# Making the low part of 109 weight tiles with an adding transfer instead of on VectorE

## The chip, the cores and the metric

One core of one Trainium2 chip runs the whole program. The metric is the device time of one execution in microseconds; lower is better.

## The reference

Two layers of a diffusion backbone over 256 latent tokens and 256 context tokens, width 1024, batch 1, all in float32. A layer normalises and modulates its tokens, then runs three branches on the result and merges them:

```python
q, k, v = h @ w_q, h @ w_k, h @ w_v          # 8 heads, each with two 64-wide halves
a = softmax(q1 k1) - lam * softmax(q2 k2)    # differential attention, axial rotary on latents
y_b = rms_norm(a @ v) @ w_attn_out
y_a = silu(layer_norm(conv31(glu(h)))) @ w_conv_out
y_c = (window_mean(h @ w_p) - h @ w_p) @ w_group @ w_pool_out
m = sum(sigmoid(h @ w_g + b_gate) * (y_a, y_b, y_c))
x = x + gate1 * rms_norm(m @ w_out)
x = x + gate2 * rms_norm((silu(h2 @ w1) * (h2 @ w2)) @ w_ffn_out)
```

The first layer does this for latent and context tokens (512 columns). The second needs the context tokens only for its keys and values, so most of its products have 256 columns.

## The kernel before

The weights lie in HBM as 302 units of 128 x 1024 float32 (512 KB), in the order of their use: the first layer's values, queries and keys (units 0 to 23), the gated convolution input "glu" (24 to 31), pooling, the three merges (to unit 76), output projection "wo" and feed-forward "fi", "fo" (77 to 150), and then the second layer, which begins with glu (151 to 158), values, queries and keys (159 to 182).

TensorE multiplies float32r operands here, so each float32 operand is kept as a pair: hi, its rounding to float32r, and lo, the rest. A product is three matmuls, hi x hi, hi x lo and lo x hi (`mm3`, L331 to L333). `prep` makes the pair of one unit: SyncE's queue loads the unit into `raw` (L295), ScalarE writes `hi = Copy(raw)` (L347) and VectorE writes `lo = raw - hi` (L348). `split` is also the helper that splits activations, so L347 and L348 stand for those too; the weight units are the rows with the names hi, lo and raw.

There are four buffers each of raw, hi and lo. `unit` calls `prep` for up to five units ahead of the one that it hands out, so a pair is made as soon as one of the four buffers of each kind is free: hi and lo come free with the last matmul of an earlier unit, raw with the last reader of the raw tile.

Nearly every changed unit is 24 matmuls (8 blocks of the contraction, three matmuls each). Where the tokens are stationary (`v_proj`, and the output projections), the weights are the moving operand, 512 columns wide. The first layer's second `v_proj` and both of the second layer take all four units at once and walk over the token tiles, so all four must be there early.

VectorE also has the softmax maxima (L704), the rotary products, the lo of every activation, and the 31 taps of the depthwise convolution (L832). In the second layer the taps are handed out in portions (`step`) between the query and key products of the attention. ScalarE has the exponentials, the copies out of PSUM and the hi of everything. GpSimd has small parts: one rotary product (L611), the lo of the keys in the second layer (L622), one channel group's taps (L829), the pooling windows and the merges' additions (L1015); it issues no transfer. `mod_close` (L400 on) turns rows of the modulation product into a gate by way of VectorE's L348 and TensorE.

The program is written in Tile: a planner walks through the instructions with its own estimate of their times and fixes each engine's order at build time, so a change of one instruction can move others. Each engine then runs its list in order and waits on semaphores.

Of the kernel before, what the change touches and what calls it, by code (L numbers as in the profile page):

```python
# [21 lines left out]
AF = mybir.ActivationFunctionType  # L22
ALU = mybir.AluOpType
# [24 lines left out]
COL_P = 4096  # L48
# [154 lines left out]
class Net:  # L203
# [85 lines left out]
    def prep(self):  # L289
        nc = self.nc  # L290
        key = self.order[self.pi]
        n = 512 if key[0] == "grp" else UW
        x = "x" if key[1] == DEPTH - 1 and key[0] in self.XK and self.pi % self.XN == 0 else ""
        raw = self.t("raw" + x, [P, UW])
        dma = nc.sync.dma_start(out=raw[:, :n], in_=self.io["w"][self.pi, :, :n])  # L295
        if x:
            self.after(self.last_dma, dma)
        self.last_dma = dma
        hi = self.t("hi" + x, [P, UW], F32R)
        lo = self.t("lo" + x, [P, UW], F32R)  # L300
        a, _ = self.split(hi[:, :n], lo[:, :n], raw[:, :n])
        if self.gate is not None and self.pi >= self.limit:
            self.after(self.gate[0], a)
            if self.pi >= self.limit + 3:
                self.gate, self.limit = None, len(self.order)
        self.prepped.append((key, hi, lo))
        self.pi += 1
# [988 lines left out]
```

## Time and profile before

| | |
|---|---|
| three runs | 1557.73 us median, 1556.97 to 1563.15 |
| profiled execution | 1556.86 us, of which the span is 1555.1 |
| TensorE busy | 1518.8 us, 98% of the span |
| VectorE, ScalarE, GpSimd busy | 974.6, 752.0 and 192.4 us |
| transfers | 236.70 MB, 152 GB/s mean |
| granted TensorE clock, mean | 0.996 of full speed |

Busy time is measured per engine inside the span, which runs from the first to the last instruction; the 1.76 us between span and execution lie around it. Matmuls overlap in the array, so a stretch in which TensorE is all busy may still hold fewer matmuls than it could.

### The profile page before, as it was taken

To read this page: it belongs to the slowest core of one execution; us is meant where nothing else is said; L and a number is where in the kernel's file an instruction comes from. 1 tells how busy PE (TensorE), PEld (TensorE's weight loads), DVE (VectorE), ACT (ScalarE), POOL (GpSimd) and SP (SyncE) were. 2 spreads that over 40 slices of the span, in tenths; PEclk is the share of its full clock that TensorE was granted. 3 is DMA by queue.
4 is the path that set the end of the run, shared out by engine and by line. 5 is a ranking of instruction groups with operands and counts; after the bars stand their busy time and mean duration, and the time that the engine had idled before them with its cause. 6 is when DMAs were issued, how large, how long until landed. Compare 5 with 4: busy or idle time off the path is not lost.

```text
span 1555.1 us, 22537 instructions
## 1 busy us (share of the span) xinstructions
PE 1518.8 (98%) x8616; PEld 1253.0 (81%) x8616; DVE 974.6 (63%) x1580; ACT 752.0 (48%) x1284; POOL 192.4 (12%) x216
## 2 busy tenths in 40 slices
PE   6999999999999999999999999998999999999998
PEld 3788878878777688877888888887789799799986
DVE  4588787999964347334333222899998656665554
ACT  5467768532353236322222221865677665554443
POOL 0000100630131100000000000054134212000000
PEclk9999999999999999999999999999999999999999
DMA  9643342232335644446322235534244675556553
GB/s 344 207 121 99 105 133 95 71 123 91 132 116 186 205 141 149 148 169 203 100 95 95 95 118 167 198 106 144 93 137 158 240 254 192 188 177 210 182 189 110
DMA packets 81693, 236.70 MB, mean 152 GB/s; under 512 B 9648, under 2 KB 18480, under 8 KB 81584
## 3 DMA queue, kind: packets, MB, share of 16 engines
q1 hardware_dynamic: 81584, 235.26, 45.7%
q8 instruction: 67, 1.10, 0.3%
q14 instruction: 42, 0.34, 0.1%
HBM read 223.69 MB, written 5.24 MB: 147 GB/s over the span
## 4 chain that ended last, share of the span: by engine, by line
PE 71%; DVE 9%; issue 1%; ACT 1%; DVEq 0%; ACTq 0%
PE psg L332 11%; PE psg L331 11%; PE psg L333 11%; PE pss L331 10%; PE pss L333 10%; PE pss L332 10%; DVE O L832 2%; PE pso L332 2%; PE pso L333 2%; PE pso L331 2%; DVE lo L348 1%; DVE Q L832 1%; PE pss L380 1%; PE pst L380 1%; PE pss L701 1%
## 5 line engine op out<-in xcount | busy, mean ns | idle before, releaser
L347 ACT ACTIVATE hi<-raw 128x1024 fp32r<-128x1024 f32 x299 | 315.2, 1056 | 528.7 <-PE psg L332 162.3
L348 DVE TENSOR_TENSOR lo<-raw,hi 128x1024 fp32r<-128x1024 f32 x299 | 375.5, 1256 | 294.0 <-ACT hi L347 290.0
L331 PE MATMUL psg<-H,hi 128*128 128x512 f32 (+1 forms) x864 | 300.0, 349 | 1.3 <-ACT H L347 0.9
L332 PE MATMUL psg<-H,hi 128*128 128x512 f32 (+1 forms) x864 | 299.4, 347 | 0.7 <-DVE H L348 0.7
L333 PE MATMUL psg<-H,lo 128*128 128x512 f32 (+1 forms) x864 | 299.5, 347 | 0.0
L331 PE MATMUL pss<-H,hi 128*128 128x256 f32 (+1 forms) x704 | 236.7, 337 | 0.1
L332 PE MATMUL pss<-H,hi 128*128 128x256 f32 (+1 forms) x704 | 235.3, 334 | 0.0
L333 PE MATMUL pss<-H,lo 128*128 128x256 f32 (+1 forms) x704 | 234.6, 333 | 0.0
L331 PEld LDWEIGHTS psg<-H,hi 128*128 128x128 f32 x864 | 162.1, 188 | 28.9 <-issue 3.2
L332 PEld LDWEIGHTS psg<-H,hi 128*128 128x128 f32 x864 | 162.4, 188 | 25.1 <-issue 3.8
L333 PEld LDWEIGHTS psg<-H,lo 128*128 128x128 f32 x864 | 162.4, 188 | 22.1 <-issue 1.8
L331 PEld LDWEIGHTS pss<-H,hi 128*128 128x128 f32 x704 | 132.2, 188 | 17.1 <-issue 2.5
L333 PEld LDWEIGHTS pss<-H,lo 128*128 128x128 f32 x704 | 133.8, 190 | 14.9
L332 PEld LDWEIGHTS pss<-H,hi 128*128 128x128 f32 x704 | 133.0, 189 | 14.0
L832 DVE SCALAR_TENSOR_TENSOR Q<-Q,perm,Q 128x482 f32<-128x482 f32 (+14 forms) x120 | 99.4, 828 | 2.5
L829 POOL TENSOR_TENSOR O<-O,tp 128x241 f32<-128x241 f32 (+14 forms) x30 | 24.6, 820 | 473.6 <-ACT tp L827 471.5
L707 ACT ACTIVATE E<-pss,st 128x512 f32<-128x512 f32 (+1 forms) x96 | 58.7, 613 | 38.1 <-DVE st L704 33.0
L1087 DVE TENSOR_TENSOR S<-pss,S 128x256 f32<-128x256 f32 (+1 forms) x43 | 23.8, 554 | 80.8 <-PE pss L333 80.8
L331 PE MATMUL psg<-V,hi 128*128 128x512 f32 (+1 forms) x192 | 64.5, 341 | 3.3 <-ACT S L1003 3.1
L1015 POOL TENSOR_TENSOR O<-O,S 128x512 f32<-128x512 f32 (+1 forms) x32 | 43.9, 1373 | 188.2 <-DVE S L1013 169.4
L332 PE MATMUL psg<-V,hi 128*128 128x512 f32 (+1 forms) x192 | 65.0, 339 | 0.8 <-DVE V L348 0.8
L333 PE MATMUL psg<-V,lo 128*128 128x512 f32 (+1 forms) x192 | 64.5, 337 | 0.0
(373 smaller groups left out, 2638.5 us busy)
## 6 DMA issues: line engine op xcount, KB each, us to landing
raw<-w SPq DMA_DIRECT2D x297, 512.0 KB, 3.4
mod<-wmod SPq DMA_DIRECT2D x66, 512.0 KB, 4.6
A<-wmod SPq DMA_DIRECT2D x18, 256.0 KB, 5.4
O<-wmod SPq DMA_DIRECT2D x16, 256.0 KB, 4.9
QD<-T SPq DMA_DIRECT2D x32, 128.0 KB, 2.4
E<-wmod SPq DMA_DIRECT2D x14, 256.0 KB, 5.3
row<-b_mod SPq DMA_DIRECT2D x24, 128.0 KB, 4.0
xs<-Q SPq DMA_DIRECT2D x12, 256.0 KB, 2.1
```

The costliest lines, as they stand in the source:

```text
L331: mm(out, sh, mh, start=start, stop=False)
L332: mm(out, sh, ml, start=False, stop=False)
L333: return mm(out, sl, mh, start=False, stop=stop)
L347: return (self.nc.scalar.activation(hi, src, AF.Copy), (lo_eng or self.nc.vector).tensor_tensor(out=lo, in0=src, in1=hi.bitcast(F32), op=A ...
L348: (lo_eng or self.nc.vector).tensor_tensor(out=lo, in0=src, in1=hi.bitcast(F32), op=ALU.subtract))
L380: ins = nc.tensor.matmul(ps[32 * kk:32 * kk + 32, 0:256], self.cc[:, k, :], raws[k], start=(k < 4), stop=(k >= 4), tile_position=(0, 32 * ...
L701: nc.tensor.matmul(pss[j][:, :n], q[a][:, j, qt * P:(qt + 1) * P], k[:, j, k0:NT], start=(a == 0), stop=(a == 1))
L707: nc.scalar.activation(e[:, :n], pss[j][:, :n], AF.Exp, bias=mx[:, j:j + 1], accum_out=ss[:, j:j + 1])
L829: nc.gpsimd.tensor_tensor(out=accs[i][:, a:b], in0=accs[i][:, a:b], in1=t, op=ALU.add)
L832: last[0] = nc.vector.scalar_tensor_tensor(out=av, in0=uv, scalar=prm[:, w:w + 1], in1=av, op0=ALU.mult, op1=ALU.add)
L1015: nc.gpsimd.tensor_tensor(out=m[:, :n], in0=m[:, :n], in1=gs[:, :n], op=ALU.add)
L1087: nc.vector.tensor_tensor(out=s[:, :n], in0=pg[:, :n], in1=s[:, :n], op=ALU.mult)
```

## The change

For 109 units, all of the first layer up to the end of its merges (0 to 76) and the second layer's glu, values, queries and keys (151 to 182), the pair is made in another way. ScalarE writes hi as before, and then also writes -raw, rounded in the same way, into lo, which so holds -hi. GpSimd then issues a transfer that reads the same unit from HBM a second time and adds it to what lies in lo, so that lo ends as raw - hi. VectorE has no part in it. The other 193 units stay as they were.

```diff
         hi = self.t("hi" + x, [P, UW], F32R)
         lo = self.t("lo" + x, [P, UW], F32R)
-        a, _ = self.split(hi[:, :n], lo[:, :n], raw[:, :n])
+        if key[0] in ("wo", "fi", "fo") or key[1] > 0 and not (
+                key[0] == "v" or key[0] == "in" and key[2] < COL_P):
+            a, _ = self.split(hi[:, :n], lo[:, :n], raw[:, :n])
+        else:
+
+            a = nc.scalar.activation(hi[:, :n], raw[:, :n], AF.Copy)
+            nc.scalar.activation(lo[:, :n], raw[:, :n], AF.Copy, scale=-1.0)
+            nc.gpsimd.dma_start(out=lo[:, :n], in_=self.io["w"][self.pi, :, :n],
+                                accum_op=ALU.add)
```

## Rows read from the trace of the kernel before

**Rows 1.** The page, part 1: the span, and busy time, share, instructions of TensorE.
```profile
span 1555.1 us, 22537 instructions
PE 1518.8 (98%) x8616; PEld 1253.0 (81%) x8616; DVE 974.6 (63%) x1580; ACT 752.0 (48%) x1284; POOL 192.4 (12%) x216
```

**Rows 2.** Windows by stage: length, busy time (instructions) by engine, clock, DMA share, GB/s.
```profile
55.00:280.00 225.00, 224.43 (x1140) 179.95 (x1139) 172.46 (x345) 152.28 (x295) 13.12 (x20) 1.00 0.38 115
...
280.00:440.00 160.00, 158.91 (x707) 125.32 (x706) 153.84 (x185) 54.08 (x74) 54.47 (x63) 1.00 0.32 107
...
1015.00:1040.00 25.00, 25.00 (x119) 20.60 (x118) 24.00 (x34) 16.51 (x33) 17.32 (x22) 1.00 0.20 66
1040.00:1120.00 80.00, 72.71 (x383) 58.28 (x382) 79.68 (x155) 45.56 (x91) 26.08 (x25) 0.98 0.35 113
```

**Rows 3.** TensorE's waits from 55 to 545 us: total, times, longest (the longest row of four).
```profile
PE psg L332 <- DVE V L348: 0.8, 1, 0.8
```

**Rows 4.** TensorE's waits in the second layer's attention, 1015 to 1215 us.
```profile
PE pst L400 <- DVE rows L348: 4.2, 2, 2.3
PE psg L331 <- ACT S L1003: 3.1, 1, 3.1
PE pss L701 <- POOL K L622: 1.7, 2, 1.5
PE pss L701 <- DVE QL L348: 0.9, 1, 0.9
```

**Rows 5.** Groups by form, whole span: count, busy us, mean ns, idle before.
```profile
L348 DVE TENSOR_TENSOR lo<-raw,hi 128x1024 fp32r<-128x1024 f32 x297 | 374.1, 1260 | 294.0 <-ACT hi L347 290.0 <-DMA raw<-w 0.2 <-PE pso L332 0.2
L347 ACT ACTIVATE hi<-raw 128x1024 fp32r<-128x1024 f32 x297 | 314.0, 1059 | 524.2 <-PE psg L332 157.7 <-issue 148.9 <-PE pss L332 95.2
```

**Rows 6.** VectorE's weight splits from 1040 to 1120 us.
```profile
L348 DVE TENSOR_TENSOR lo<-raw,hi 128x1024 fp32r<-128x1024 f32 x12 | 15.1, 1256 | 0.0
```

**Rows 7.** VectorE's and ScalarE's weight splits from 55 to 280 us.
```profile
L348 DVE TENSOR_TENSOR lo<-raw,hi 128x1024 fp32r<-128x1024 f32 x30 | 36.6, 1221 | 6.2 <-ACT hi L347 5.7 <-PE pso L332 0.2
...
L347 ACT ACTIVATE hi<-raw 128x1024 fp32r<-128x1024 f32 x29 | 30.7, 1057 | 10.7 <-PE psg L332 8.1 <-PE pso L333 2.1
```

**Rows 8.** A GpSimd addition by form; the page's weight loads with us to landing.
```profile
L1015 POOL TENSOR_TENSOR O<-O,S 128x512 f32<-128x512 f32 x16 | 25.1, 1569 | 112.5 <-DVE S L1013 96.8 <-DMA E<-wmod 9.5 <-DVE perm L426 6.2
...
raw<-w SPq DMA_DIRECT2D x297, 512.0 KB, 3.4
```

**Rows 9.** Weight loads (L295) issued in the first 60 us: us to landing.
```profile
DMA to landing us min/median/max: 3.4/6.5/8.4
```

**Rows 10.** Windows of the start and just behind it, columns as in Rows 2.
```profile
15.00:50.00 35.00, 33.05 (x211) 18.37 (x212) 15.81 (x41) 16.26 (x27) 0.00 (x0) 1.00 1.02 369
50.00:55.00 5.00, 5.00 (x24) 4.04 (x23) 3.09 (x6) 2.62 (x5) 0.00 (x0) 1.00 0.17 58
```

**Rows 11.** Timeline of unit 0: start, length; its lo, a load's issue, its first matmul with lo.
```profile
18.39 1.22 DVE L348 TENSOR_TENSOR lo<-raw,hi 128x1024 fp32r<-128x1024 f32 x1
...
21.56 0.33 SPq L295 DMA_DIRECT2D raw<-w  x1
...
23.75 0.39 PE L332 MATMUL psg<-lo,H 128*128 128x512 f32 x1
```

**Rows 12.** Timeline of unit 15, last of the first layer's second values: its lo, first matmuls with lo.
```profile
117.78 1.21 DVE L348 TENSOR_TENSOR lo<-raw,hi 128x1024 fp32r<-128x1024 f32 x1
...
120.10 0.63 PE L332 MATMUL psg<-lo,H 128*128 128x512 f32 x2
```

**Rows 13.** Timeline of units 155 (glu) and 162 (values) of the second layer: lo, first matmul.
```profile
998.65 1.23 DVE L348 TENSOR_TENSOR lo<-raw,hi 128x1024 fp32r<-128x1024 f32 x1 [1.26 <-ACT hi L347]
...
1003.60 0.28 PE L333 MATMUL psg<-H,lo 128*128 128x256 f32 x1
...
1016.93 1.22 DVE L348 TENSOR_TENSOR lo<-raw,hi 128x1024 fp32r<-128x1024 f32 x1 [0.40 <-ACT hi L347]
...
1019.73 0.39 PE L332 MATMUL psg<-lo,H 128*128 128x512 f32 x1
```

## The prediction

> **What bounds the kernel now.** I began with the page's busy times. TensorE is busy 1518.8 of 1555.1 us; VectorE, which the change relieves, 974.6 [rows 1]. So 36 us of the span are open to any gain at all, and work taken off VectorE is worth only what it takes out of TensorE's waits. I looked for those by stage. From 55 to 440 us, the first layer's attention and half of its merges, TensorE is busy 224.43 of 225 and 158.91 of 160 us, although VectorE is busy 77% of the one stretch and 96% of the other [rows 2]. The longest total among its waits there is 0.8 us [rows 3]. A saturated VectorE costs nothing in that layer. The second layer's attention is different: from 1040 to 1120 us VectorE is busy 79.68 of 80 us and TensorE 72.71, and the granted clock has fallen to a mean of 0.98 of full speed [rows 2]. TensorE waits there for VectorE's rows of a gate (4.2 us), for ScalarE's sigmoid (3.1), for GpSimd's lo of the keys (1.7) and for VectorE's lo of the queries (0.9) [rows 4]. That is where VectorE is worth something.
>
> **What the change removes.** 109 of VectorE's splits at 1260 ns are 137 us [rows 5]. In the first layer I give them nothing, because TensorE hardly waits (above). In the stretch from 1040 to 1120 us, 12 of them take 15.1 of VectorE's 79.68 us [rows 6, 2], so its backlog shrinks by a fifth. Of the waits in rows 4, those for VectorE and GpSimd come to 4.2 + 1.7 + 0.9 = 6.8 us. They are waits for a result behind other work in an engine's list, so a shorter list should cut them and not end them: I take half, 3.4 us. The bounds are nothing, and all of rows 4 with the clock, 9.9 + 0.02 x 80 = 11.5 us.
>
> **What it adds on ScalarE.** A second pass per unit at 1059 ns [rows 5], 115 us in all. From 55 to 280 us some 30 units bring 32 us [rows 7] to the 152.28 that ScalarE has [rows 2]: 184 of 225 us, 82%. VectorE stands at 77% in that stretch today and TensorE does not wait for it, so I take nothing; what covers it is the work of another head that TensorE has beside each softmax. Without that cover, 82% could cost some 5 us. The raw buffer now comes free after two ScalarE passes (2.12 us) where it took a ScalarE and a VectorE pass (2.32 and VectorE's queue), so SyncE's loads start no later.
>
> **What it adds in the chain of one unit.** Before, lo is there 1.22 us after VectorE starts on it [rows 11]. Now come ScalarE's pass (1.06), GpSimd's issue, and a transfer of 512 KB that reads HBM, reads lo and writes lo. The kernel before issues no transfer from GpSimd, so both parts are bounded. The issue: no less than SyncE's 0.33 [rows 11], no more than GpSimd's addition of 512 columns, 1.57 [rows 8]; I take 1.0, about midway. The landing: a weight load's median of 3.4 us [rows 8] below, the slowest load of the crowded start, 8.4 [rows 9], above; I take 1.5 x 3.4 = 5.1, for three streams where a load has two. So lo is later by 1.06 + 1.0 + 5.1 - 1.22 = 5.9 us, with bounds of 3.6 (0.33 and 3.4) and 9.8 (1.57 and 8.4).
>
> The Trainium skill, "DMA: Bandwidth & Descriptors", section "Anatomy of one DMA", puts a transfer from GpSimd at 2.0 us plus its bytes at 436 GB/s; no run here shows one. An estimate by that page is 3.2 us for issue and landing together, 3.0 us of delay in place of 5.9, and a sum near no change.
>
> **Where the delay reaches TensorE.** With four buffers a unit has up to three units of TensorE's time between its buffer and its use, and mostly that covers it. I laid each unit's lo beside its first matmul and looked for less than 5.9 us:
> - Unit 155, in the second layer's glu, where a unit has 256 columns and so takes half the time: lo ends at 999.88, its first use is at 1003.60 [rows 13]. 3.7 us of cover, 5.9 - 3.7 = 2.2 us lost.
> - Unit 162, the last of the four that the value product takes together right behind: lo ends at 1018.15, used at 1019.73 [rows 13]. 1.6 us of cover, 4.3 us lost.
> - Unit 15, the same place in the first layer: lo ends at 118.99, used at 120.10 [rows 12]. 1.1 us of cover, 4.8 us short. Here attention's matmuls are interleaved and the planner can move some ahead: I take half, 2.4.
> - The start. From 15 to 50 us the transfer engines are full (share 1.02, 369 GB/s), then nearly idle (0.17) [rows 10]. Four units' second reads, 4 x 524,288 bytes at 369 GB/s, are 5.7 us in front of the modulation weights that TensorE needs next. Unit 0 has 4.1 us of cover (19.61 to 23.75) [rows 11] and loses 1.8 more. Between nothing, if the four fit in gaps of the queue, and 7.5 I take 4.
>
> That the start pays for second reads on another queue at all is read from its full share [rows 10]. The Trainium skill, "DMA: Bandwidth & Descriptors", section "Issuing engines are not separate DMA queues", says the same of all transfers: whichever engine issues them, they run on the same 16 engines. By that rule the start would pay the whole 5.7, and the sum be 1.7 higher.
>
> Elsewhere the second reads have room: 30 units at 1.42 us are 43 us of the 225 from 55 to 280, a share of 0.38 that becomes 0.57 [rows 2, 10].
>
> GpSimd's list gets an instruction that waits for ScalarE's second pass. Behind it stand the rotary products, the keys' lo and the merges' additions, and for these wait VectorE and then TensorE's scores. I price that at nothing beyond the issue, since TensorE is a head ahead; the rest of it is in the upper bound.
>
> **The sum.** Lost: 2.2 + 4.3 + 2.4 + 4 = 12.9 us. Gained: 3.4. Net 9.5 on the profiled execution's 1556.86 (span 1555.1): 1566 us. The median of the runs, 1557.73, lies 0.9 above that execution, well inside what I can resolve. I take 0.5%, 7.8 us, as about what a measurement of this kernel can tell from no change.
>
> **The rivals.**
> - *VectorE's relief decides* (the other side). Place: 1040 to 1120 us. If the taps no longer crowd out the rows and the splits, all of rows 4 and the lost clock come back, 11.5 us. With a delay of 3.6 the losses are unit 162's 2.0 and half of unit 15's 2.5, 3.2 together: 8.3 us faster, 1548.6. At a delay of 5.9 this gain is eaten (12.9 lost), so it decides below about 5. For it: VectorE's 79.68 of 80. Against: 3.1 of rows 4 hang on ScalarE, which gets more work.
> - *A slow transfer.* At 9.8 us of delay, by crowding or by GpSimd's list, unit 155 loses 6.1, unit 162 8.2, unit 15 8.7 and the start 5.7 + 5.7: 34.4 us, 1591. For it: loads of the same size do take 8.4 when the engines are full. Against: they are not full at units 155 and 162.
> - *The transfer is hidden anyway.* At 3.6 us the same 3.2 us are lost and half of the waits, 3.4, come back: 1556.7. The Trainium skill's figure in "DMA: Bandwidth & Descriptors" (above) would lead here.
>
> **How the numbers follow.** I give the forecast case 0.40, with a range of its own from 1560 to 1573; about two thirds of that is slower by over 0.5%, the rest within. The slow transfer gets 0.15, all slower. The hidden transfer gets 0.19, all within. VectorE's relief gets 0.26, all faster. So faster 0.26, within 0.5% 0.13 + 0.19 = 0.32, slower 0.27 + 0.15 = 0.42. The range reaches from a little beyond the relief, 1546, to the slow transfer, 1591; what lies outside is the stronger half of the one and the worse part of the other, under 2 in 10.
>
> **What would show it.** VectorE's weight splits fall from 302 to 193, ScalarE's passes over raw rise by 109, and GpSimd has 109 issues whose row gives the landing: near 5.1 us if I am right, near 3.4 or over 8 for the rivals. TensorE should show new waits, for ScalarE or a transfer of lo, at 23 us, near 1003 and 1019, and at the first layer's second values. From 1040 to 1120 us VectorE should drop from 79.68 of 80 to some 65, and the wait for rows should shrink. I am wrong if TensorE's idle time at those four places does not grow, if its waits in the second attention go altogether, or if a stage that I priced at nothing (ScalarE in the first attention, GpSimd's list) holds the difference.

## The result and the profile after

The changed kernel takes 1612.4 us (median of four runs, 1610.28 to 1612.57) where the kernel before takes 1558.05: a ratio of 1.034, interval 1.032 to 1.036. It is 54 us slower, outside my range and beyond the worst of my rivals (1591). The profiled execution is 1610.28 us with a span of 1608.5.

The page of the changed kernel, parts 1, 3 (queue: packets, MB, share of 16 engines), 5 and 6 (last column: us from issue to landing):

```profile
span 1608.5 us, 22739 instructions
PE 1536.8 (96%) x8616; PEld 1260.1 (78%) x8616; DVE 856.3 (53%) x1471; ACT 851.4 (53%) x1394; POOL 276.8 (17%) x325
...
q1 hardware_dynamic: 81584, 235.26, 43.5%
q0 software_dynamic: 15696, 56.89, 19.1%
...
L308 POOL DMA_DIRECT2D lo<-w x109 | 95.4, 875 | 899.5 <-ACT lo L307 437.4
...
raw<-w SPq DMA_DIRECT2D x297, 512.0 KB, 4.0
lo<-w POOLq DMA_DIRECT2D x108, 512.0 KB, 8.3
...
QD<-T SPq DMA_DIRECT2D x32, 128.0 KB, 6.4
```

VectorE did lose its work: 974.6 us [rows 1] became 856.3. The span grew by 53 us. Of these, 35 are idle time of TensorE (72 us outside its busy time, where 36 were), and 18 are the same 8616 matmuls taking longer. The mean granted clock fell from 0.996 to 0.989 of full speed; by an estimate from these means and the two spans that is worth about 11 us, part of it in idle time. Two lines name suspects. Queue q0 carries the adding transfers: 56.89 MB for 19.1% of the 16 engines' span, while q1 moves 235.26 MB for 43.5%. Per MB that is 0.336% against 0.185%. And lo lands 8.3 us after its issue, not the 5.1 that I took.

Windows of the changed kernel, in the columns of [rows 2] (busy time by engine, granted clock, DMA share, GB/s):

```profile
15.00:50.00 35.00, 30.42 (x189) 14.51 (x185) 10.35 (x34) 20.18 (x32) 4.45 (x5) 0.95 1.05 350
55.00:280.00 225.00, 210.48 (x1024) 166.64 (x1023) 125.39 (x281) 160.68 (x290) 38.14 (x48) 0.98 0.73 181
280.00:440.00 160.00, 154.74 (x718) 121.19 (x718) 135.65 (x187) 87.22 (x127) 60.48 (x83) 0.98 0.74 170
1085.00:1165.00 80.00, 70.72 (x367) 57.10 (x366) 71.29 (x141) 52.18 (x97) 33.61 (x36) 0.94 0.69 172
```

From 55 to 280 us TensorE is busy for 210.48 of 225 us, where it had 224.43 [rows 2]: this stage, which I had called safe, loses most. Its DMA share went from 0.38 to 0.73; I had written 0.57. The last line is the stretch of [rows 2] at 1040 to 1120, moved by the 45 us that TensorE is late there: VectorE is relieved (71.29 of 80, before 79.68), yet TensorE does less than before. Its longest waits there are 6.6 us for a gate that VectorE makes (G, L418, next table) and 2.2 us for an exponential.

TensorE's longest waits in the changed kernel, whole span:

```profile
PE pss L709 <- ACT E L715: 11.2, 3, 6.0
...
PE psg L341 <- DMA lo<-w: 7.9, 6, 2.5
PE pss L709 <- DVE G L418: 6.6, 1, 6.6
PE pst L777 <- ACT row L355: 3.7, 2, 2.6
PE pst L778 <- DVE row L356: 2.9, 2, 2.7
```

The largest is no wait for a weight: the scores (L709) wait for an exponential on ScalarE (L715), 6.0 us at once. The timeline of the changed kernel around it (start, length, engine, line; in brackets the idle time ahead and its releaser) shows why:

```profile
95.70 3.05 SPq L640 DMA_DIRECT2D QD<-T  x4
95.82 0.88 POOL L308 DMA_DIRECT2D lo<-w  x1 [0.65 <-ACT lo L307]
...
106.94 1.06 ACT L355 ACTIVATE QH<-QD 128x1024 fp32r<-128x1024 f32 x1 [9.23 <-DMA QD<-T]
107.91 0.67 ACT L715 ACTIVATE E<-pss,st 128x512 f32<-128x512 f32 x1
108.03 1.22 DVE L356 TENSOR_TENSOR QL<-QD,QH 128x1024 fp32r<-128x1024 f32 x1 [9.13 <-ACT QH L355]
108.72 0.58 PE L709 MATMUL pss<-K,QH 128*128 128x256 f32 x1 [5.97 <-ACT E L715]
```

At 95.70 SyncE issues the four small transfers that stack a head's rotated queries on chip (QD, L640; in the kernel before L632). At 95.82 GpSimd issues an adding transfer. ScalarE's next instruction in its list splits the queries and waits 9.23 us for them. Behind it in the list stands the exponential, ready but not reachable, and for that TensorE's next scores wait 5.97 us. Three engines stand still behind 512 KB of queries that are already on the chip. The rest of the 11.2 us are two such waits, of 3.0 and 2.2 us, each behind a query split that waited for its transfer (4.85 and 3.91 us). While the four transfers were under way the transfer engines were full (next to last number of a row):

```profile
98.00:100.00 2.00, 2.00 (x10) 1.61 (x9) 0.90 (x3) 0.00 (x0) 0.25 (x1) 1.00 0.99 202
100.00:102.00 2.00, 2.00 (x11) 1.66 (x10) 0.00 (x0) 0.00 (x0) 0.00 (x0) 1.00 1.03 221
102.00:104.00 2.00, 0.75 (x4) 0.27 (x2) 0.00 (x0) 0.00 (x0) 0.00 (x0) 1.00 1.09 247
```

That this is crowding shows in the transfers of one stretch, 50 to 150 us, in both kernels. Before:

```profile
q1 hardware_dynamic: 4467, 11.47, 38.1%
...
raw<-w SPq DMA_DIRECT2D x13, 512.0 KB, 3.7
mod<-wmod SPq DMA_DIRECT2D x4, 512.0 KB, 4.2
QD<-T SPq DMA_DIRECT2D x16, 128.0 KB, 2.4
```

After:

```profile
q1 hardware_dynamic: 5062, 12.29, 40.6%
q0 software_dynamic: 1811, 6.57, 34.5%
...
raw<-w SPq DMA_DIRECT2D x12, 512.0 KB, 9.7
lo<-w POOLq DMA_DIRECT2D x11, 512.0 KB, 8.7
QD<-T SPq DMA_DIRECT2D x16, 128.0 KB, 8.0
mod<-wmod SPq DMA_DIRECT2D x2, 512.0 KB, 15.1
```

q1 costs the same per MB as before (3.3% each), the adding queue 5.25%. Every other transfer of the stretch lands later: queries 8.0 us instead of 2.4, weights 9.7 instead of 3.7. Over the whole stretch the engines have idle time (mean share 0.75), but a small transfer meets the load of its own few microseconds, and that was full.

To see where the time goes I laid the first matmul of each unit beside that of the kernel before, both measured from the start of the span. TensorE is late by these us (columns: the changed kernel and experiments told below):

```
unit                     before at  after  e1    e2    e4    e5    e6    e16
1   values                  37.8    +8.1  -2.2  +5.3  +1.2  +1.0  +7.7  -0.3
8   keys, first head        84.6    +9.6  -3.9  +3.0  +1.2  +2.3  +5.7  +1.0
12  second values          114.0   +21.1  -6.1  +4.3  +2.4 +15.3  +5.8  +1.2
15                         119.6   +21.9  -6.9  +4.5  +2.4 +15.5  +5.8  +1.1
38  first merge            314.4   +26.1  +3.4  +7.2  +2.4 +21.4  +9.7  +5.2
39                         321.4   +33.5  +3.2 +11.1  +2.7 +29.0 +18.2 +14.3
78  output projection      553.5   +37.1  +1.0 +10.8  +2.7 +35.2 +21.0 +20.0
151 second layer, glu      990.3   +37.9  +1.8 +11.6  +3.5 +35.9 +21.8 +20.8
158                       1012.9   +43.8  +9.2 +18.3 +20.0 +49.5 +28.0 +34.6
162 last of four values   1019.5   +45.0  +9.2 +18.6 +19.9 +49.0 +27.9 +34.1
301 last unit             1546.0   +53.3  +9.5 +17.6 +25.3 +61.9 +31.9 +40.2
```

In the changed kernel: 8.1 us at the start, 11.5 between units 8 and 12, where the first heads' queries are stacked, 7.4 at one place, unit 39, 5.9 in the second glu, 8.3 after unit 162, and some 12 in small pieces between. Not every step of the table is a loss: work that the planner put elsewhere shows too, as in e1, where the -6.9 at unit 15 is +0.1 at unit 16.

### The profile page after: what moved, and what is told of

Its sections match the earlier page's. It is cut to its first block, busy times and chain, and to the rows that moved or that the text cites. A ratio compares the mean times of both kernels' runs of the same rounds, so it can differ in the third digit from the quotient of the medians.

```text
span 1608.5 us, 22739 instructions
## 1 busy us (share of the span) xinstructions
PE 1536.8 (96%) x8616; PEld 1260.1 (78%) x8616; DVE 856.3 (53%) x1471; ACT 851.4 (53%) x1394; POOL 276.8 (17%) x325
## 3 DMA queue, kind: packets, MB, share of 16 engines
q1 hardware_dynamic: 81584, 235.26, 43.5%
q0 software_dynamic: 15696, 56.89, 19.1%
## 4 chain that ended last, share of the span: by engine, by line
PE 71%; DMA 8%; DVE 8%; issue 6%; ACT 5%; SPq 1%; POOL 0%; DVEq 0%; ACTq 0%; POOLq 0%
PE psg L339 11%; PE psg L341 11%; PE psg L340 11%; PE pss L339 9%; PE pss L341 9%; PE pss L340 9%; DVE O L840 2%; PE pso L340 2%; DMA QD<-T 2%; DMA lo<-w 2%; PE pso L339 2%; PE pso L341 2%; DVE Q L840 2%; DMA mod<-wmod 1%; PE pst L388 1%
## 5 line engine op out<-in xcount | busy, mean ns | idle before, releaser
L355 ACT ACTIVATE hi<-raw 128x1024 fp32r<-128x1024 f32 x190 | 200.2, 1056 | 372.3 <-issue 153.7
L356 DVE TENSOR_TENSOR lo<-raw,hi 128x1024 fp32r<-128x1024 f32 x190 | 235.5, 1242 | 240.1 <-ACT hi L355 235.5
L308 POOL DMA_DIRECT2D lo<-w x109 | 95.4, 875 | 899.5 <-ACT lo L307 437.4
L339 PEld LDWEIGHTS psg<-H,hi 128*128 128x128 f32 x864 | 164.1, 190 | 35.4 <-issue 5.8
L340 PEld LDWEIGHTS psg<-H,hi 128*128 128x128 f32 x864 | 164.1, 190 | 24.6 <-issue 2.5
L306 ACT ACTIVATE hi<-raw 128x1024 fp32r<-128x1024 f32 (+1 forms) x109 | 114.4, 1050 | 114.7 <-PE psg L340 65.9
L307 ACT ACTIVATE lo<-raw 128x1024 fp32r<-128x1024 f32 (+1 forms) x109 | 113.7, 1043 | 9.6 <-PE pso L340 5.7
L715 ACT ACTIVATE E<-pss,st 128x512 f32<-128x512 f32 (+1 forms) x96 | 58.7, 613 | 18.5 <-DVE st L712 14.1
```

What stands on the lines that cost most here:

```text
L306: a = nc.scalar.activation(hi[:, :n], raw[:, :n], AF.Copy)
L307: nc.scalar.activation(lo[:, :n], raw[:, :n], AF.Copy, scale=-1.0)
L308: nc.gpsimd.dma_start(out=lo[:, :n], in_=self.io["w"][self.pi, :, :n], accum_op=ALU.add)
L339: mm(out, sh, mh, start=start, stop=False)
L340: mm(out, sh, ml, start=False, stop=False)
L355: return (self.nc.scalar.activation(hi, src, AF.Copy), (lo_eng or self.nc.vector).tensor_tensor(out=lo, in0=src, in1=hi.bitcast(F32), op=A ...
```

## The experiments

Each ratio is to the kernel before, with its 95% interval; the kernel before lies between 1556.9 and 1558.4 us in all of them. Edits are to the changed kernel unless said otherwise.

**The transfer taken away, and made plain.** e1 and e2 part ScalarE's second pass, the plain second read and the adding.

```diff
 e1
-            nc.gpsimd.dma_start(out=lo[:, :n], in_=self.io["w"][self.pi, :, :n],
-                                accum_op=ALU.add)
 e2
-            nc.gpsimd.dma_start(out=lo[:, :n], in_=self.io["w"][self.pi, :, :n],
-                                accum_op=ALU.add)
+            nc.gpsimd.dma_start(out=lo[:, :n], in_=self.io["w"][self.pi, :, :n])
```

> Leaves out the adding transfer alone: lo stays at -hi, so its time counts and its numbers do not. If the transfers cost the 54 us, by their own lateness or by what they hold up, this runs at 1548 to 1560 us. If ScalarE's second pass or the new order of the lists costs it, this stays above 1590.

> The same transfer as a plain copy: it writes the unit over lo and adds nothing. The bytes from HBM, the queue and GpSimd's list are those of the change. If the adding makes a packet take twice as long on the transfer engines (0.19 of the engines' span for 56.89 MB, against 0.435 for 235.26 MB), about half of the loss goes: 1575 to 1590 us. If the number of bytes or GpSimd's list is what costs, it stays at 1605 to 1612.

e1: 1565.94 us, 1.0049 [1.0033, 1.0064], between its two expectations. e2: 1576.6 us, 1.0120 [1.0104, 1.0136]. The page of e2, the plain transfer's queue and landings over the whole span:

```profile
q0 software_dynamic: 15696, 56.89, 10.6%
...
lo<-w POOLq DMA_DIRECT2D x108, 512.0 KB, 5.1
...
QD<-T SPq DMA_DIRECT2D x32, 128.0 KB, 3.4
```

The same packets and bytes from the same queue take 10.6% of a span of 1572.8 us when copied, 167 us, and 19.1% of 1608.5 when added, 307 us: 1.84 times. Adding instead of copying costs 35.8 of the 54 us. The plain landing, 5.1 us, is by chance the one I had estimated for the adding transfer.

Without any transfer the changed kernel is still 8 us slower than before, and the table puts 7 of them between units 151 and 158. There TensorE waits once for the glu's sigmoid on ScalarE, 4.7 us. TensorE's waits in e1:

```profile
PE psg L337 <- ACT S L793: 6.0, 2, 4.7
PE pss L707 <- POOL K L628: 3.8, 2, 2.5
```

**No lo at all.** e9 leaves out ScalarE's second pass too and reads hi in lo's place (the line that takes lo's tile moves into the other branch, not shown).

```diff
-            nc.scalar.activation(lo[:, :n], raw[:, :n], AF.Copy, scale=-1.0)
-            nc.gpsimd.dma_start(out=lo[:, :n], in_=self.io["w"][self.pi, :, :n],
-                                accum_op=ALU.add)
+            lo = hi
```

> Leaves out the making of lo for the 109 units altogether: no VectorE split, no second ScalarE pass, no transfer, and the matmuls read hi in its place, so its time counts and its numbers do not. It is what VectorE's relief would be worth for nothing. If the second attention waits for VectorE: 1545 to 1553. If nothing does: 1556 to 1560, and the 8 us by which the kernel without the adding transfer (1566) stood above before are ScalarE's second pass.

1550.59 us, 0.9943 [0.9922, 0.9963]. VectorE's relief, had for nothing, is worth 7.8 us against the kernel before of the same runs (6 to 12 by the interval), and the waits for lo, which e9 has none of, are in that. From e9 to e1, ScalarE's second pass costs 15.4.

**ScalarE's pass given to VectorE.** -raw is written by VectorE, the rest as changed.

```diff
-            nc.scalar.activation(lo[:, :n], raw[:, :n], AF.Copy, scale=-1.0)
+            nc.vector.tensor_scalar(lo[:, :n], raw[:, :n], -1.0, None, op0=ALU.mult)
```

> The changed kernel with -raw written into lo by VectorE (one input) instead of a second ScalarE pass. Against the run without any lo (1551), ScalarE's pass alone stood at 1566, 15 us. If that pass is dear because of its place in ScalarE's list, about 10 us come back here: 1600 us. If its cost only looked so because nothing else was late in those runs, no change: 1608 to 1614.

1612.22 us, 1.0352 [1.0336, 1.0367]: the total does not change. With the adding transfer there, the place of the pass does not matter to it; TensorE's longest waits of e13 are now for lo and for the keys that GpSimd makes:

```profile
PE psg L341 <- DMA lo<-w: 11.6, 8, 2.9
PE pss L709 <- POOL K L630: 10.1, 2, 6.5
```

So the 15.4 of e1 and the transfer's cost are not two terms that can be moved one by one: with ScalarE freed of the pass, other waits took its place.

**Queries without transfers.** e6 stacks them by four copies on VectorE; e7 does that in the kernel before, as a control.

```diff
-                nc.sync.dma_start(out=d[64 * r:64 * r + 64, j, :n],
-                                  in_=q[64 * j:64 * j + 64, :n])
+                nc.vector.tensor_copy(d[64 * r:64 * r + 64, j, :n],
+                                      q[64 * j:64 * j + 64, :n])
```

> The changed kernel with the queries stacked by four VectorE copies of 64 partitions instead of four transfers (QD). Those small transfers took 6.4 us to land where they took 2.4 before. If the adding transfers cost by holding them up, 14 to 20 us come back: 1592 to 1598. If the lateness of lo itself or ScalarE's list is what costs, 1608 to 1614.

> The control for the run with copied queries: the same four copies in the kernel before. Their transfers were not late there, so no theory gives them more than a few us: 1553 to 1562.

e6: 1590.13 us, 1.0199 [1.0172, 1.0226], 22 us less than the changed kernel. e7: 1556.62 us, 0.9993 [0.9982, 1.0003]. The copies are worth nothing before and 22 us after, so the queries' late transfers hold that much. The table shows where: between units 8 and 12 e6 loses 0.1 us where the changed kernel lost 11.5. TensorE's waits of e6 from 55 to 320 us hold no scores:

```profile
PE psg L339 <- ACT S L795: 1.2, 1, 1.2
PE psg L341 <- DMA lo<-w: 0.8, 1, 0.8
```

e6 also takes the queries' own 6 MB off the engines, so its 22 us hold a little relief of the other transfers too.

**The same copies with the plain transfer.** e15 joins the edits of e6 and e2.

> Copied queries (1590 with adding transfers) and the transfer as a plain copy that adds nothing. If what is left of the loss is again the longer packets, through lo itself and the modulation loads, it goes to 1566 to 1576, near the 1566 of the kernel without the transfer. If the query transfers were all that the longer packets hurt, it stays at 1584 to 1592.

1573.0 us, 1.0107 [1.0092, 1.0122]. With a plain transfer the copies give 3.6 us (from e2), with the adding one 22. And adding costs 17.1 us with copied queries (1573.0 to 1590.13), 35.8 without: half of what adding costs reaches TensorE through the queries.

**Another queue for the queries.** Is it SyncE's list that holds them up? e14 issues them from ScalarE's queue.

```diff
-                nc.sync.dma_start(out=d[64 * r:64 * r + 64, j, :n],
+                nc.scalar.dma_start(out=d[64 * r:64 * r + 64, j, :n],
```

> The changed kernel with the query-stacking transfers (QD) issued from ScalarE's queue instead of SyncE's, everything else the same. If they are late because they stand behind weight loads in SyncE's queue, they land in 2.5 to 4 us again and 10 to 20 us come back: 1592 to 1602. If they are late because the 16 engines are shared with the adding packets, they stay at 5 us or more and the time at 1605 to 1616.

1621.96 us, 1.0420 [1.0396, 1.0444], slower than either theory expected. The page's landing row for them:

```profile
QD<-T ACTq DMA_DIRECT2D x32, 128.0 KB, 6.1
```

6.1 us against 6.4: from issue to landing, the queue makes no difference. The Trainium skill, "DMA: Bandwidth & Descriptors", section "Issuing engines are not separate DMA queues", says that all of them end on the same 16 engines and interleave there, and this row agrees. Why it is 10 us slower was not followed up; the issues now stand in ScalarE's list.

**One stage alone.** e3 changes units 0 to 76, e4 151 to 182, e8 36 to 76, each by its own bounds in `prep`, as in e4:

```diff
-        if key[0] in ("wo", "fi", "fo") or key[1] > 0 and not (
-                key[0] == "v" or key[0] == "in" and key[2] < COL_P):
+        if not 151 <= self.pi <= 182:
```

> Only units 0 to 76 by transfer, the second layer as before. In the changed kernel TensorE was 37 us late when the first layer's merges were done, so if the stages add up: 1595 us.

> Only units 151 to 182 by transfer, the first layer as before. The rest of the lateness, 16 us, if the stages add up: 1574 us. If VectorE's relief in the second attention were worth something by itself, under 1570.

> Only units 36 to 76, the first layer's merges, by transfer. No query transfers run there, units have 8 to 18 us of cover, and VectorE is at 95%. By the lateness of lo alone nothing is lost: 1556 to 1560. In the changed kernel TensorE fell 11 us further behind over this stretch (7.4 of it where the second half of the heads is normalised), so if the transfers do that by themselves: 1565 to 1570.

e3: 1594.11 us, 1.0236 [1.0218, 1.0254], 36.0 more than before, as expected. e4: 1582.32 us, 1.0165 [1.0143, 1.0187], 24.2 more, where the table's 16 (53.3 less 37.1) had been expected. e8: 1569.13 us, 1.0080 [1.0063, 1.0097], 11.7 more. Alone the second layer loses 16.5 us in its glu, against 5.9 in the changed kernel. The timeline of e4 has the reason, two long waits of TensorE, and its windows the granted clock (the next to last three numbers of a row are clock, DMA share, GB/s):

```profile
1013.25 0.58 PE L340 MATMUL psg<-H,lo 128*128 128x256 f32 x1 [4.10 <-DMA lo<-w]
1023.30 0.58 PE L338 MATMUL psg<-H,hi 128*128 128x256 f32 x1 [3.67 <-ACT S L794]
```

```profile
1000.00:1010.00 10.00, 9.15 (x77) 8.94 (x76) 3.11 (x11) 8.98 (x15) 1.72 (x2) 1.00 0.75 207
1010.00:1020.00 10.00, 6.38 (x30) 6.18 (x30) 2.34 (x5) 4.33 (x7) 1.73 (x2) 0.66 1.05 269
1020.00:1030.00 10.00, 6.70 (x36) 6.02 (x36) 2.57 (x5) 7.07 (x12) 0.86 (x1) 0.66 0.75 179
```

The waits come to 7.8 us. Behind each of them the granted clock stood at 1.2 GHz while TensorE was busy for 11.6 us in all, which by an estimate is 5.8 us more. Some 3 of the 16.5 us stay unexplained. e8's extra includes 6.1 us at unit 39.

**The start undone.** e5 gives units 0 to 3 back to VectorE; e16 does so with copied queries.

```diff
+        if not (4 <= self.pi <= 76 or 151 <= self.pi <= 182):
```

> The changed kernel with units 0 to 3 back on VectorE, so that no adding transfer runs while the start fills the transfer engines. TensorE was 8 us late at unit 1 in the changed kernel: if the start's share is paid in full, 1604 us. If later waits swallow it, 1609 to 1612.

> Copied queries and units 0 to 3 back on VectorE. Undoing the start alone changed nothing (1615 against 1612). If a later wait for queries had swallowed it there, it shows here: 1581 to 1585. If the start is worth nothing by itself: 1588 to 1593.

e5: 1615.39 us, 1.0363 [1.0338, 1.0388]. e16: 1597.26 us, 1.0261 [1.0234, 1.0288], 7 us slower than e6. Both miss. In both the start's 7 to 8 us are saved (unit 1 at +1.0 and -0.3), and in both they are lost again, mostly in the second glu: 13.6 and 13.8 us between units 151 and 158. TensorE's waits of e16 there, 1000 to 1060 us, are those of e4:

```profile
PE psg L340 <- DMA lo<-w: 4.2, 1, 4.2
PE psg L338 <- ACT S L794: 3.7, 1, 3.7
```

**GpSimd as the giver.** As a better version of the idea, e10 makes lo of ten late units (odd ones from 163 to 181) on GpSimd in the kernel before.

```diff
+        a, _ = self.split(hi[:, :n], lo[:, :n], raw[:, :n],
+                          nc.gpsimd if 163 <= self.pi <= 182 and self.pi % 2 else None)
```

> The kernel before, with lo of every other unit of the second layer's attention (163 to 181) subtracted on GpSimd instead of VectorE. VectorE's relief for nothing was worth 8 us over both layers, some 2 to 4 of it in this stretch, where GpSimd is busy 26 of 80 us. If GpSimd's 3 us for such a subtraction can be hidden: 1553 to 1557. If it delays the keys' lo behind it: 1560 to 1566.

1566.86 us, 1.0061 [1.0046, 1.0076], slower: TensorE now waits once, 5.8 us, for the keys that GpSimd makes. The timeline of e10 shows GpSimd's subtraction just ahead, and beside it a VectorE addition in the keys' chain that took 2.56 us instead of 0.41:

```profile
1074.48 0.41 DVE L613 TENSOR_TENSOR T<-T,sh 128x256 f32<-128x256 f32 x1
...
1079.06 2.51 POOL L349 TENSOR_TENSOR lo<-raw,hi 128x1024 fp32r<-128x1024 f32 x1
...
1079.30 2.56 DVE L613 TENSOR_TENSOR T<-T,sh 128x256 f32<-128x256 f32 x1
```

No kernel here that computes the whole result beats the one before; e7 equals it.

## Why the prediction was wrong

The direction I gave the highest chance, slower, came true, but mostly by a path that the sum did not hold; the time did not. In steps of the runs, the way from 1558 to 1612 is: relief -7.8 (e9), ScalarE's second pass +15.4 (e1), plain second reads with their issues on GpSimd +10.7 (e2), adding +35.8.

- **The step that failed: "Elsewhere the second reads have room".** I priced a unit's second read at 1.42 us of the engines, the rate of plain loads at the start, and then asked only whether the sum fits: 0.38 and 0.19. Two things were wrong. An adding transfer takes 1.84 times the engine time of a copy, and the share became 0.73. And a mean share below 1 is not the condition, because the engines were full for microseconds at a time (0.99 to 1.09 from 98 to 106 us): the queries' transfers, which ScalarE's list waits for in order, landed in 6.4 us instead of 2.4, and 8.0 in the first attention. e6 against e7 prices the queries at 22 us. No rival had this. My rows showed what stood at stake in units; I never asked which other transfers the path waits for.
- **The delay of one lo.** The issue was taken as 1.0 us and is 0.88; ScalarE's pass 1.06, and is 1.05. The landing was taken as 5.1 and is 8.3, next to the upper bound of 8.4. By my sum that is 1.05 + 0.88 + 8.3 - 1.22 = 9.0 us instead of 5.9; since a landing is counted from the start of its issue, my sum has the issue twice, and the delay itself is 8.1. A landing over 8 was the sign that I gave for the slow transfer, but that rival's whole price, 34.4 us at 9.8, lay at the same four places. I counted three streams as one and a half loads; the plain transfer alone takes 5.1. The Trainium skill, "DMA: Bandwidth & Descriptors", section "Anatomy of one DMA", leads to an estimate of 3.2 us for this size. Even the plain transfer of e2 measures 5.1 beside this kernel's other traffic, so here the measurement decides.
- **The places where the delay reaches TensorE.** Start: taken 4, found 8.1; the crowded start pays the whole second read and more. Second glu (unit 155): taken 2.2, found 5.9 from unit 151 to 158, and up to 16.5 in e4. Unit 162: taken 4.3, found 1.2. Unit 15: taken 2.4, found 0.8. Together 12.9 taken and 16.0 found. As a list of places this held, and it was 30% of the matter. But the start's term can't be had back alone: in e5 and e16 the gain is lost downstream.
- **ScalarE's second pass, priced at nothing.** Shown to cost 15.4 us without transfers (e9 to e1), 7 of them at the second glu's sigmoid, a place that I had looked at only for lo. My bound of 5 was for the first attention alone. That GpSimd's list costs nothing was not tested by itself; in e2 it and the plain second reads together cost 10.7 us. With the transfer there, moving the pass gives nothing (e13).
- **VectorE's relief.** Taken as 3.4 with bounds of 0 and 11.5; e9 gives 7.8. In e9's trace TensorE is 3.8 us ahead of the kernel before at unit 151, so part of this comes in the first layer, where I had given nothing. VectorE drops from 79.68 to 71.29 of 80 us, not to 65.
- **Unit 39** was not in the sum. In the changed kernel a row that TensorE waits for stands in VectorE's list behind four taps and a reciprocal of 3.34 us; 7.4 us are lost there, 6.1 when only units 36 to 76 are changed (e8), 0 without transfers (e1). That the planner's order does it is read from the timeline and was not tested.

Left open: e6 still loses 32 us to before. ScalarE's pass (e1, 8 net of relief), the plain reads (7, e15 less e1) and the remaining cost of adding (17.1) add up to them, but which of lo's own lateness, the modulation loads and the changed lists carries how much was not parted. Nor is it settled why the second glu loses 6 us in one kernel and 14 to 17 in others; in the others it is the same two waits (lo 3.9 to 4.2 us, sigmoid 3.7), with the lower clock behind them in e4 (above).

## What to carry to other kernels

A transfer that computes on its way is to be priced by the engine time that it takes, not by its bytes, and a stage's mean DMA share below 1 does not make it free: look for the small transfers that stand on the critical chain of the same stage, and for what waits behind their reader in an in-order list. Test such a suspicion by taking the small transfers away in the changed kernel and in the old one. Work moved from an engine that is saturated but little waited for has little to give: here 7.8 us at best, against 61.9 of price.

## What the hardware showed that I had not expected

- Adding 512 KB from HBM to a tile took 1.84 times the engine time of copying it (19.1% of 1608.5 us against 10.6% of 1572.8, 56.89 MB each) and landed in 8.3 us against 5.1.
- On-chip transfers of 128 KB landed in 2.4 us before, 3.4 beside plain second reads and 6.4 beside adding ones, whichever queue issued them (6.1 from ScalarE's).
- After TensorE had stood still for 6 us, the granted clock was at 1.2 GHz (0.50, second line below) and the matmul at 108.72 took 0.58 us, where one of the same form took 0.28 at 101.19. The changed kernel's windows:

```profile
104.00:106.00 2.00, 0.00 (x0) 0.00 (x0) 0.00 (x0) 0.00 (x0) 0.00 (x0) 0.75 1.07 254
106.00:108.00 2.00, 0.00 (x0) 0.00 (x0) 0.00 (x0) 1.06 (x2) 0.00 (x0) 0.50 0.58 201
```
